# First layer norm's modulation weights loaded in four units of two feature tiles, with the first four projection tiles computed between the units

## The chip, the cores and the metric

The kernel runs on one core of one Trainium2 chip. The metric is device time in microseconds (us) of one execution; lower is better. Engines are named as in the profile: PE (TensorE, matmuls), PEld (its weight loads), DVE (VectorE), ACT (ScalarE), POOL (GpSimd) and SP (SyncE, which issues nearly all DMA transfers).

## The reference, cut to what matters

Two layers run over 256 latent tokens and 256 context tokens of width 1024. Each sub-layer begins with an RMS norm whose result is scaled and shifted by vectors that come from the conditioning vector `c` (latent tokens) or `c_ctx` (context tokens) through `mod_w`. This case is about the very first such norm and the projection `even_w_in` behind it:

```python
mod = silu(c) @ mod_w[0] + mod_b[0]          # 6 vectors of 1024: shift, scale, gate, shift, scale, gate
h   = x * rsqrt(mean(x * x) + EPS) * norm_g  # per token, over the 1024 features
h   = h * (1 + scale) + shift                # modulate
p   = h @ even_w_in                          # 1024 x 3328: a_q, a_k, a_v, b_q, b_ff, b_fb, b_i, b_g
```

The first projection tiles are the attention key and query (`a_k`, `a_q`), the value (`a_v`), then the inputs of the recurrent heads. Everything later (attention, recurrence, output projection, FFN, the second layer) stays as it is.

## The kernel before, in words

Features lie on the 128 partitions, tokens in the free dimension: 8 feature tiles k of 128 features by 512 tokens (latent 0:256, context 256:512). All dense products are done in three matmuls per weight block and feature tile: activations and weights are each split into a rounded part (`hi`) and the rest (`lo`), and hi*hi, lo*hi and hi*lo are added in PSUM. The split of activations gives the tiles `hh` and `hl`; the split of weights gives `whi` (ACT, line 268) and `wlo` (DVE, line 269). Weights arrive as pieces of 8 blocks of 128x128 (512 KB, tile `raw`) in the order in which `take` asks for them; `ensure` splits pieces up to LOOK = 2 ahead.

The program's first stage is written in a fixed order (`tc.manual_schedule`); there each engine runs its instructions in the order of the code. Before the change this stage does:

- SP loads constants, `x` (8 latent tiles of 128 KB, 4 context tiles of 256 KB), then `mod_w`'s columns for scale and shift of the first norm as 32 tiles of 256 KB: four quarters `nt` of 8 tiles (one for each feature tile of the contraction); the quarters are scale features 0:512, scale 512:1024, shift 0:512, shift 512:1024. Then come the first raw pieces.
- ACT and DVE square and sum `x`, PE sums over the partitions (line 453), ACT takes Ln and Exp for the reciprocal root: first for latent tokens, then for context tokens.
- `mod0a(nt)` (line 175) is 8 matmuls of fp32, which PE runs as 16 rows of the trace, on four column groups at once, followed by a copy to SBUF on ACT (line 178). `mod0b(nt)` (line 185) is 4 small matmuls (8 rows) that turn the result onto the partitions; `mod_finish` (lines 154 and 158, DVE) adds the bias and makes `gsv` = (1 + scale) * norm_g. A quarter of scale or shift serves four feature tiles.
- `Norm.scaled` (line 459, DVE) multiplies x by `gsv` and the root; `Norm.shifted` adds the shift and splits: `hh` on ACT (line 465), `hl` on DVE (line 466). All four quarters are done before the first `shifted`.

Behind this stage the work is ordered by `group`, which goes on PE in program order and gives, after every TICK = 1600 columns, one step to each lane (`q`: attention) and to the further modulation vectors (`mod_tick`, one task per MODE ticks; most tasks are two DVE reductions of 1.22 us, line 233). The group `p1` computes the output tiles a_k and a_q's first tile, for latent and context tokens apart (96 matmuls of 256 columns); `p2` computes the other three tiles of a_q and a_v (96 matmuls of 512 columns). `qk_post` (lines 567 and 578 on PE) follows a tile. `tokgroup` (lines 409 to 411) comes next with 96 matmuls of 512 columns.

Of the kernel before, what the change touches and what calls it, by code (L numbers as in the profile page):

```python
# [16 lines left out]
P = 128  # L17
D = 1024
# [22 lines left out]
MODE = 2.3  # L41
# [27 lines left out]
def hybrid_kernel(ctx, tc, xT, wst, mw0, mwT, small, cbc, cst, imask, dmat, out, order):  # L69
# [35 lines left out]
    x = [cp.tile([P, L], F32, tag=f"x{k}", name=f"x{k}") for k in range(KD)]  # L105
    xc = [u((P, 2, L)) for _ in range(KD // 2)]
    for k in range(KD):
        nc.sync.dma_start(x[k][:], xT[:, k, LAT])
    for k in range(KD // 2):
        nc.sync.dma_start(xc[k][:], xT[:, 2 * k:2 * k + 2, CTX])  # L110

    def xs(k, s):
        return x[k][:] if s == 0 else xc[k // 2][:, k % 2, :]

    con0 = [u() for _ in range(3)]
    mws = []
    for i in range(32):
        if 16 <= i < 22:
            if i % 2 == 0:
                pair = rawp.tile([P, 2, NT], F32, tag="raw", name=nm("raw"))  # L120
            t = pair[:, i % 2, :]
        elif 22 <= i < 28:
            if i % 2 == 0:
                pair = mp.tile([P, D], F32, tag="mr", name=nm("mr"))
            t = pair[:, (i % 2) * NT:(i % 2 + 1) * NT]
        elif i < 16:
            t = u()[:]
        else:
# [42 lines left out]
    def mod0a(nt):  # L171
        ps = axb()
        for k in range(KD):
            g = k % 4
            T.matmul(ps[32 * g:32 * g + 32, :], cT[:, k, :], mws[nt * 8 + k], start=(k < 4), stop=(k >= 4),  # L175
                     skip_group_check=True)
        parts[nt] = u()
        A.activation(parts[nt][:], ps[:], AF.Copy)

    def mod0b(nt):  # L180
        ch, half = 1 - nt // 2, nt % 2
        part = parts[nt]
# [3 lines left out]
        mod_finish(0, ch, half * 4, half * 4 + 4, ps2[:].rearrange("p c s -> p s c"))  # L186
# [73 lines left out]

    def ensure(p):
        for q in range(len(pieces), min(p + LOOK, N_PIECE - 1) + 1):
            r = q
            load_raw(r)
            src = raws.pop(r)
# [153 lines left out]
    class Norm:  # L419
# [6 lines left out]
        def pre(self, k):  # L426
# [5 lines left out]
            A.activation(hi[:, LAT], x[k][:], AF.Copy, scale=g)  # L432
            V.scalar_tensor_tensor(lo[:, LAT], x[k][:], g, hi[:, LAT].bitcast(F32), ALU.mult, ALU.subtract)
# [50 lines left out]

    manual[0] = True
    with tc.manual_schedule():
        h = new_h()
        ns = [Norm(0, 0, s, h) for s in range(2)]
        for n in ns:
            for k in range(KD):  # L490
                n.add(k)
            n.stats()
        for r in range(3):
            load_raw(r)
        ts_ = [u() for _ in range(KD)]
# [16 lines left out]
        mod0b(3)  # L512
        for i, t in enumerate(con0):
            nc.sync.dma_start(t[:], cst[:, N_KEEP + i * NT:N_KEEP + (i + 1) * NT])
        nc.sync.dma_start(con[:, C_RCOS:], cst[:, C_RCOS:N_KEEP])
        nc.sync.dma_start(msk[:], imask)
        nc.sync.dma_start(cb[:], cbc.rearrange("s d -> (s d)").unsqueeze(0).partition_broadcast(P).rearrange("p o (s d) -> p (o s) d", s=2))
        for n in ns:
            for k in range(KD):
                if n.s == 0 and k in (1, 4):  # L520
                    ensure(k // 4 - LOOK)
                n.shifted(k, ts_[k][:, n.sl])
# [9 lines left out]

    omh = cp.tile([P, 4], F32, tag="omh", name="omh")
    nomh = cp.tile([P, 4], F32, tag="nomh", name="nomh")
    lbh = cp.tile([P, 4], F32, tag="lbh", name="lbh")
    l0, l1 = sml[:, S_LB:S_LB + 4], sml[:, S_LB + 4:S_LB + 8]
    mx, e0, e1 = sm(4), sm(4), sm(4)
    V.tensor_tensor(mx, l0, l1, ALU.max)
# [775 lines left out]
```

## Time and profile before

| what | value |
|---|---|
| median of the runs | 1154.58 us (1154.38 to 1154.76, 3 runs) |
| profiled execution, its own time | 1153.62 us |
| its span in the trace | 1151.9 us |
| PE busy / weight loads / DVE / ACT | 1123.6 / 1002.4 / 766.5 / 554.1 us |
| mean granted TensorE clock | 0.996 of full speed |
| PE in the first 20 us | 2.2 us busy |

The span is the trace from first to last instruction; the 1.7 us between it and the execution's own time lie around it. PE's ends are modelled, so a busy PE is not PE at its peak. The window views below give busy time of each engine in a stretch, the granted clock (1.00 is the upper of TensorE's two levels, 2.4 GHz; 0.50 the lower, 1.2 GHz) and what the DMA engines moved.

### The profile page before, as it was taken

What the parts mean: (1) busy time and instruction counts of PE and PEld (TensorE: products, weight loads), DVE (VectorE), ACT (ScalarE), POOL (GpSimd) and SP (SyncE); (2) the same over time, 40 slices, a digit from 0 to 9 for tenths busy, and PEclk for the clock granted to TensorE, in tenths of its full rate; (3) what the DMA queues carried; (4) which work ended last, traced back from release to release, by engine and by line L of the source; (5) the groups of instructions that cost most, each with busy time, mean ns of one, the idle gap of its engine ahead of it and who ended that gap; (6) DMA issues with size and microseconds to landing.
All of it is one profiled execution on the core that took longest, in us unless ns stands there. A gap on an engine that the chain in (4) does not pass through costs nothing.

```text
span 1151.9 us, 18864 instructions
## 1 busy us (share of the span) xinstructions
PE 1123.6 (98%) x7514; PEld 1002.4 (87%) x7514; DVE 766.5 (67%) x1399; ACT 554.1 (48%) x948; POOL 20.8 (2%) x46
## 2 busy tenths in 40 slices
PE   3999999999999999999999998999999999999998
PEld 1777878888998888888888898999999999999998
DVE  3878699789889557347884568373646577555553
ACT  5776667573763322132232466454445657543441
POOL 0012000000000000000000000000000000000000
PEclk9999999999999999999999999999999999999999
DMA  9976212225327446236884323343424265655553
GB/s 333 343 231 183 92 58 72 96 89 163 112 86 261 147 147 213 81 128 215 314 300 139 98 86 116 112 134 116 139 101 146 92 198 161 194 183 184 183 183 109
DMA packets 56121, 182.46 MB, mean 158 GB/s; under 512 B 6368, under 2 KB 9824, under 8 KB 55904
## 3 DMA queue, kind: packets, MB, share of 16 engines
q1 hardware_dynamic: 53648, 176.45, 46.9%
q0 software_dynamic: 2240, 4.72, 1.7%
q8 instruction: 59, 0.97, 0.3%
q14 instruction: 30, 0.25, 0.1%
q10 hardware_dynamic: 144, 0.08, 0.0%
HBM read 177.56 MB, written 1.05 MB: 155 GB/s over the span
## 4 chain that ended last, share of the span: by engine, by line
PE 90%; DVE 6%; ACT 2%; issue 1%; DMA 1%; DVEq 0%; ACTq 0%; SPq 0%
PE mm L338 24%; PE mm L336 24%; PE mm L337 24%; PE ax L337 2%; PE ax L336 2%; PE ax L338 2%; DVE wlo L269 1%; PE ax L175 1%; PE ax L656 1%; PE ax L675 1%; PE ax L777 1%; DVE u L459 1%; PE mm L411 1%; PE mm L409 1%; PE mm L410 1%
## 5 line engine op out<-in xcount | busy, mean ns | idle before, releaser
L268 ACT ACTIVATE whi<-raw 128x1024 fp32r<-128x1024 f32 x230 | 243.2, 1058 | 385.9 <-PE mm L337 222.4
L269 DVE TENSOR_TENSOR wlo<-raw,whi 128x1024 fp32r<-128x1024 f32 x230 | 280.7, 1222 | 167.5 <-ACT whi L268 166.8
L336 PE MATMUL mm<-hh,whi 128*128 128x256 f32 (+1 forms) x1072 | 362.4, 339 | 1.2 <-ACT whi L268 0.9
L338 PE MATMUL mm<-hh,wlo 128*128 128x256 f32 (+1 forms) x1072 | 361.3, 337 | 0.6 <-DVE wlo L269 0.6
L337 PE MATMUL mm<-hl,whi 128*128 128x256 f32 (+1 forms) x1072 | 361.4, 337 | 0.1
L336 PE MATMUL mm<-u,whi 128*128 128x256 f32 (+2 forms) x768 | 236.3, 309 | 1.1 <-DVE x L483 1.1
L337 PE MATMUL mm<-u,whi 128*128 128x256 f32 (+2 forms) x768 | 236.9, 309 | 0.0
L338 PE MATMUL mm<-u,wlo 128*128 128x256 f32 (+2 forms) x768 | 236.7, 308 | 0.0
L338 PEld LDWEIGHTS mm<-hh,wlo 128*128 128x128 f32 x1072 | 204.3, 191 | 21.9 <-DVE wlo L269 0.8
L336 PEld LDWEIGHTS mm<-hh,whi 128*128 128x128 f32 x1072 | 204.1, 191 | 21.6 <-ACT whi L268 0.9
L337 PEld LDWEIGHTS mm<-hl,whi 128*128 128x128 f32 x1072 | 204.2, 191 | 20.2 <-DVE hl L466 0.3
L336 PEld LDWEIGHTS mm<-u,whi 128*128 128x128 f32 x768 | 146.4, 191 | 8.7 <-issue 1.3
L337 PEld LDWEIGHTS mm<-u,whi 128*128 128x128 f32 x768 | 146.6, 191 | 7.1
L338 PEld LDWEIGHTS mm<-u,wlo 128*128 128x128 f32 x768 | 146.5, 191 | 7.1
L233 DVE CUSTOM_DVE_ANT_0 mr<-mr,cb 128x1024 f32<-128x1024 f32 x72 | 87.1, 1222 | 16.1 <-DMA mr<-in_mwT_dram 15.4
L416 ACT ACTIVATE u<-u 128x512 fp32r<-128x512 f32 (+1 forms) x84 | 43.0, 526 | 46.9 <-DVE u L1002 26.9
L1002 DVE TENSOR_TENSOR u<-u,mm 128x512 f32<-128x512 f32 (+1 forms) x40 | 22.1, 553 | 43.2 <-PE mm L338 43.2
L417 DVE TENSOR_TENSOR u<-u,u 128x512 fp32r<-128x512 f32 (+1 forms) x84 | 46.5, 565 | 5.1 <-ACT u L416 5.1
L233 DVE CUSTOM_DVE_ANT_0 u<-mr,cb 128x1024 bf16<-128x1024 f32 x40 | 48.3, 1219 | 2.2 <-ACT cb L524 1.2
L336 PE MATMUL ax<-u,u 128*128 128x256 f32 x160 | 45.9, 287 | 3.1 <-ACT u L416 3.1
L483 DVE SCALAR_TENSOR_TENSOR x<-mm,modv,x 128x256 f32<-128x256 f32 x48 | 22.3, 480 | 36.1 <-PE mm L338 36.1
L337 PE MATMUL ax<-u,u 128*128 128x256 f32 x160 | 46.0, 287 | 0.0
(220 smaller groups left out, 1233.8 us busy)
## 6 DMA issues: line engine op xcount, KB each, us to landing
raw<-in_wst_dram SPq DMA_DIRECT2D x230, 512.0 KB, 3.6
mr<-in_mwT_dram SPq DMA_DIRECT2D x80, 512.0 KB, 4.5
u<-in_mw_dram SPq DMA_DIRECT2D x16, 256.0 KB, 5.2
u<-u POOLq DMA_DIRECT2D x20, 128.0 KB, 5.3
u<-in_dmat_dram POOLq DMA_DIRECT2D x8, 256.0 KB, 3.1
raw<-in_mw_dram SPq DMA_DIRECT2D x6, 256.0 KB, 5.2
mr<-in_mw_dram SPq DMA_DIRECT2D x6, 256.0 KB, 5.2
x<-in_xT_dram SPq DMA_DIRECT2D x8, 128.0 KB, 3.3
```

What stands on the lines that cost most here:

```text
L175: T.matmul(ps[32 * g:32 * g + 32, :], cT[:, k, :], mws[nt * 8 + k], start=(k < 4), stop=(k >= 4), skip_group_check=True)
L233: V.tensor_tensor_reduce(o, mr[:], cb[:, s, :], 1.0, 0.0, ALU.mult, ALU.add, mvec(l, s, ch, k))
L268: A.activation(hi[:], src[:], AF.Copy)
L269: V.tensor_tensor(lo[:], src[:], hi[:].bitcast(F32), ALU.subtract)
L336: T.matmul(o, w[0], a[0], start=first, stop=False, skip_group_check=shared)
L337: T.matmul(o, w[0], a[1], start=False, stop=False, skip_group_check=shared)
L338: anchor[0] = T.matmul(o, w[1], a[0], start=False, stop=last, skip_group_check=shared)
L409: T.matmul(ps[t][:], a[0], w[0], start=(k == 0), stop=False)
L416: A.activation(hi, src, AF.Copy)
L417: V.tensor_tensor(lo, src, hi.bitcast(F32), ALU.subtract)
L483: V.scalar_tensor_tensor(xs(m, s), ps[:, sl], mvec(l, s, ch, m), xs(m, s), ALU.mult, ALU.add)
L1002: V.tensor_tensor(g[:, 0:w], g[:, 0:w], ps[2 * i + 1][:, 0:w], ALU.mult)
```

## The change

The modulation weights of the first norm are regrouped on the host: unit p (of four) holds the scale columns and the shift columns of feature tiles 2p and 2p+1, so that after one unit two feature tiles can be finished. Unit 0 is now loaded ahead of `x`. The statistics use squares of 512 columns and two accumulating matmuls per stream, and one ACT table that holds both Ln and Exp. The first four output tiles (a_k and a_q's first three tiles, now all `p1`, 512 columns wide) are taken k by k inside the written order: `dense(k, ...)` with the three matmuls of each tile, `mod0a` and `mod0b` of the next unit between them. During this stage a weight piece (two k of four tiles) is split when its unit comes (`look[0] = 0`). The constants of the recurrent gates (`lb_consts`) move into the stage. `p2` keeps two tiles, and MODE goes from 2.3 to 1.5.

```diff
-MODE = 2.3
+MODE = 1.5
...
+    mw_load(0)
+    for j in range(2):
+        nc.sync.dma_start(xl[j][:], xT[:, 0, 4 * j:4 * j + 4, :])
     for k in range(KD // 2):
-        nc.sync.dma_start(xc[k][:], xT[:, 2 * k:2 * k + 2, CTX])
+        nc.sync.dma_start(xc[k][:], xT[:, 1, 2 * k:2 * k + 2, :])
...
+        for i, ch in enumerate((1, 0)):
+            mod_finish(0, ch, 2 * p, 2 * p + 2, ps2[:, 2 * i:2 * i + 2, :].rearrange("p c s -> p s c"))
...
-        mod0a(0)
-        mod0a(1)
-        mod0b(0)
-        scaled(0, range(4))
-        mod0a(2)
-        mod0b(1)
-        scaled(0, range(4, 8))
-        scaled(1, range(4))
-        mod0a(3)
-        mod0b(2)
-        scaled(1, range(4, 8))
-        mod0b(3)
...
+        load_raw(0)
+        for p in range(1, 3):
+            mw_load(p)
+            load_raw(p)
+            if p == 1:
+                mod0a(0)
+                mod0b(0)
+                lb_consts()
+                for n in ns:
+                    xx = xl if n.s == 0 else xc
+                    sq = []
+                    for j in range(4):
+                        q = u((P, 2, L))
+                        A.activation(q[:], xl[j // 2][:, 2 * (j % 2):2 * (j % 2) + 2, :] if n.s == 0 else xc[j][:], AF.Square)
+                        if j:
+                            V.tensor_tensor(sq[0][:], sq[0][:], q[:], ALU.add)
+                        sq.append(q)
+                    ps = axb()[:, 0:L]
+                    for j in range(2):
+                        T.matmul(ps, ones, sq[0][:, j, :], start=(j == 0), stop=(j == 1))
+                    n.r = u()[:, 0:L]
+                    A.activation(n.r, ps, AF.Ln, bias=epst[:], scale=1.0 / D)
+                    A.activation(n.r, n.r, AF.Exp, scale=-0.5)
...
+        def dense(k, js):
+            for j in js:
+                w = take('ein', k, j)
+                o = p1[j][:]
+                T.matmul(o, w[0], HS[k][0], start=(k == 0), stop=False)
+                T.matmul(o, w[0], HS[k][1], start=False, stop=False)
+                anchor[0] = T.matmul(o, w[1], HS[k][0], start=False, stop=(k == KD - 1))
+
+        for p in range(4):
+            k = 2 * p
+            ts = [scaled(k)]
+            ensure(p)
...
+            shifted(k, ts[0])
+            ts.append(scaled(k + 1))
+            shifted(k + 1, ts[1])
+            dense(k, range(4))
+            if p < 3:
+                mod0a(p + 1)
+            dense(k + 1, range(2))
+            if p < 3:
+                mod0b(p + 1)
+            dense(k + 1, range(2, 4))
...
-    p1 = group('ein', [E_AK, E_AQ], K8, HS, sls=(LAT, CTX))
     start('q', qk_post([(p1[0], 1, kt), (p1[1], 0, qt)]))
-    p2 = group('ein', [E_AQ + 1, E_AQ + 2, E_AQ + 3, E_AV], K8, HS, kouter=False)
-    start('q', qk_post([(p2[j], 0, qt) for j in range(3)]))
-    start('q', v_post(p2[3]))
+    start('q', qk_post([(p1[2], 0, qt), (p1[3], 0, qt)]))
+    p2 = group('ein', [E_AQ + 3, E_AV], K8, HS, kouter=False, banks=[axb(), mmb()])
+    start('q', qk_post([(p2[0], 0, qt)]))
+    start('q', v_post(p2[1]))
```

ACT's queue at the start of the changed program; line 172 copies `mod0a(0)`, 490 to 492 belong to `lb_consts`, 517 are squares of x, 525 and 526 are Ln and Exp of a stream:

```order
L160 ACTIVATE cT<-sml 128x8x2
...
L172 ACTIVATE u_177<-ax_168 128x512
L490 ACT_TABLE_LOAD
L491 ACTIVATE s_188<-s_188 128x4
L492 ACTIVATE s_189<-s_189 128x4
L517 ACTIVATE u_202<-x_86 128x512
...
L525 ACTIVATE u_216<-ax_213,eps 128x256
L526 ACTIVATE u_216<-u_216 128x256
L517 ACTIVATE u_219<-u_88 128x512
...
L525 ACTIVATE u_233<-ax_230,eps 128x256
L526 ACTIVATE u_233<-u_233 128x256
L263 ACTIVATE whi_261<-raw_148 128x1024
```

Before, the same queue began its squares (line 445) straight behind the two small Exps, and the copies of `mod0a` (line 178) stood behind both streams' Exp (line 456):

```order
L541 ACTIVATE s_413<-s_413 128x4
L542 ACTIVATE s_414<-s_414 128x4
L1037 ACTIVATE idr<-con 128x128
L445 ACTIVATE u_199<-x_86 128x256
...
L290 ACTIVATE u_253<-ax_251,eps 128x256
L456 ACT_TABLE_LOAD
L456 ACTIVATE u_253<-u_253 128x256
L178 ACTIVATE u_280<-ax_271 128x512
L178 ACTIVATE u_291<-ax_282 128x512
```

So the copy of `mod0a(0)` and the constants' Exps moved ahead of all squares.

PE's queue of the changed program at the end of unit 0; line 178 is `mod0b(1)`, lines 544 to 546 are `dense(1, ...)` with hh_134 and then `dense(2, ...)` with hh_136:

```order
L544 MATMUL mm_255<-hh_134,whi_261 128x512
L545 MATMUL mm_255<-hl_135,whi_261 128x512
L546 MATMUL mm_255<-hh_134,wlo_262 128x512
L178 MATMUL ax_329<-con,u_321 128x2 x4
L544 MATMUL mm_256<-hh_134,whi_261 128x512
L545 MATMUL mm_256<-hl_135,whi_261 128x512
L546 MATMUL mm_256<-hh_134,wlo_262 128x512
L544 MATMUL mm_257<-hh_134,whi_261 128x512
L545 MATMUL mm_257<-hl_135,whi_261 128x512
L546 MATMUL mm_257<-hh_134,wlo_262 128x512
L544 MATMUL mm_254<-hh_136,whi_346 128x512
L545 MATMUL mm_254<-hl_137,whi_346 128x512
```

Before, the last two `mod0b` (line 185) stood together, and the first dense matmuls (line 336) came right behind them:

```order
L185 MATMUL ax_341<-con,u_313 128x2 x4
L185 MATMUL ax_351<-con,u_339 128x2 x4
L336 MATMUL mm_431<-hh_183,whi_365 128x256
L336 MATMUL mm_432<-hh_183,whi_365 128x256
L337 MATMUL mm_431<-hl_184,whi_365 128x256
```

Each of the three later `mod0b` now has six dense matmuls behind it before the first matmul that needs its result.

DVE's queue at the same place of the changed program, from `mod_finish` of unit 1 (lines 147, 151) over `scaled` (454) and the piece's `wlo` (264) to `hl` (461):

```order
L147 TENSOR_TENSOR modv<-ax_329,sml 128x2x2
L151 SCALAR_TENSOR_TENSOR gsv<-modv,sml 128x2x2
L147 TENSOR_TENSOR modv<-ax_329,sml 128x2x2
L454 SCALAR_TENSOR_TENSOR u_343<-x_86,gsv,u_216 128x256
L454 SCALAR_TENSOR_TENSOR u_343<-u_89,gsv,u_233 128x256
L264 TENSOR_TENSOR wlo_347<-raw_166,whi_346 128x1024
L461 SCALAR_TENSOR_TENSOR hl_137<-u_343,modv,hh_136 128x256 x2
```

This sequence now stands once in every unit; before, `scaled` of all tiles stood ahead of the last `mod_finish`.

## Rows read from the trace of the kernel before

**Rows 1.** The page, first part: busy time, share of the span, instructions.

```profile
PE 1123.6 (98%) x7514; PEld 1002.4 (87%) x7514; DVE 766.5 (67%) x1399; ACT 554.1 (48%) x948; POOL 20.8 (2%) x46
```

**Rows 2.** The chain that ended last, first 45 us: start, us, what.

```profile
19.00 1.22 PE ax L453 x2
20.22 5.53 PE ax L175 x32
25.75 0.98 PE ax L185 x8
26.73 2.00 PE ax L175 x16
...
29.72 4.18 PE ax L175 x16
...
38.33 0.80 PE mm L338 x2
```

**Rows 3.** Timeline of PE, three stretches: start, us, line, operation, tiles, count.

```profile
50.73 0.40 PE L336 MATMUL mm<-hh,whi 128*128 128x512 f32 x1
...
75.20 0.39 PE L409 MATMUL mm<-whi,hh 128*128 128x512 f32 x1
...
78.38 0.39 PE L411 MATMUL mm<-whi,hl 128*128 128x512 f32 x1
78.61 2.73 PE L567 MATMUL ax<-u,u 128*128 128x512 f32 x6
...
87.33 1.69 PE L578 MATMUL ax<-u,u 128*128 128x256 f32 x6
```

**Rows 4.** DMA: an issue group (time to landing last), SP's timeline, a window.

```profile
con<-in_cst_dram SPq DMA_DIRECT2D x1, 129.0 KB, 2.6
...
7.00 10.65 SPq L130 DMA_DIRECT2D u<-in_mw_dram  x16
...
14.00:16.00 2.00, 0.00 (x0) 0.00 (x0) 0.55 (x2) 1.99 (x7) 0.00 (x0) 1.00 1.05 406
```

**Rows 5.** Timeline of ACT: Ln, Exp, a copy, a weight split, 12 of `hh`.

```profile
12.49 0.47 ACT L290 ACTIVATE u<-ax,eps 128x256 f32<-128x256 f32 x1 [1.82 <-PE ax L453]
...
14.28 0.42 ACT L456 ACTIVATE u<-u 128x256 f32<-128x256 f32 x1
...
23.93 0.60 ACT L178 ACTIVATE u<-ax 128x512 f32<-128x512 f32 x1 [1.48 <-PE ax L175]
...
37.68 1.04 ACT L268 ACTIVATE whi<-raw 128x1024 fp32r<-128x1024 f32 x1
38.63 4.89 ACT L465 ACTIVATE hh<-u,modv 128x256 fp32r<-128x256 f32 x12
```

**Rows 6.** Timeline of DVE: `mod_finish`, `scaled`, a weight split, 12 of `hl`, two 512-wide.

```profile
26.77 0.17 DVE L154 TENSOR_TENSOR modv<-ax,sml 128x8 f32<-128x8 f32 x1 [7.83 <-PE ax L185]
...
27.18 1.67 DVE L459 SCALAR_TENSOR_TENSOR u<-x,gsv,u 128x256 f32<-128x256 f32 x4
...
37.06 1.21 DVE L269 TENSOR_TENSOR wlo<-raw,whi 128x1024 fp32r<-128x1024 f32 x1
...
40.52 4.83 DVE L466 SCALAR_TENSOR_TENSOR hl<-u,modv,hh 128x256 fp32r<-128x256 f32 x12
...
61.78 1.42 DVE L573 SCALAR_TENSOR_TENSOR u<-u,sml,u 128x512 f32<-128x512 f32 x2 [2.53 <-ACT u L572]
```

**Rows 7.** Windows (PE, PEld, DVE, ACT, POOL busy, granted clock, DMA) and two PE waits.

```profile
36.60:41.20 4.60, 3.88 (x17) 3.47 (x18) 4.60 (x10) 4.60 (x11) 0.00 (x0) 0.63 1.03 411
...
706.90 0.58 PE L336 MATMUL ax<-u,u 128*128 128x256 f32 x1 [3.13 <-ACT u L416]
...
708.00:710.00 2.00, 2.00 (x11) 2.00 (x11) 2.00 (x3) 1.98 (x4) 0.00 (x0) 0.50 0.00 0
...
933.61 0.35 PE L336 MATMUL mm<-u,whi 128*128 128x256 f32 x1 [1.08 <-DVE x L483]
...
934.00:936.00 2.00, 2.00 (x19) 2.00 (x18) 1.71 (x5) 2.00 (x6) 0.00 (x0) 1.00 0.85 285
```

More of the change, by code (lines that the diff above doesn't have):

```diff
@@ L169, in hybrid_kernel, with mod0a @@
     parts = {}
-    def mod0a(nt):
+    def mod0a(p):
         ps = axb()
@@ L174, in mod0a, with mod0b @@
             g = k % 4
-            T.matmul(ps[32 * g:32 * g + 32, :], cT[:, k, :], mws[nt * 8 + k], start=(k < 4), stop=(k >= 4),
+            T.matmul(ps[32 * g:32 * g + 32, :], cT[:, k, :], mws[p][k][:], start=(k < 4), stop=(k >= 4),
                      skip_group_check=True)
[L177 to L182, printed above, removed]
+        parts[p] = u()
+        A.activation(parts[p][:], ps[:], AF.Copy)
+    def mod0b(p):
+        part = parts[p]
         ps2 = axb((P, 4, 2))
@@ L259, in load_raw @@
             raws[r] = t
+    look = [0]
     def ensure(p):
[L262 to L265, printed above, removed]
+        for q in range(len(pieces), min(p + look[0], N_PIECE - 1) + 1):
+            load_raw(q)
+            src = raws.pop(q)
             hi = wp.tile([P, PIECE, P], F32R, tag="whi", name=nm("whi"))
@@ L483, in upd, with lb_consts @@
         V.scalar_tensor_tensor(xs(m, s), ps[:, sl], mvec(l, s, ch, m), xs(m, s), ALU.mult, ALU.add)
+    omh = cp.tile([P, 4], F32, tag="omh", name="omh")
+    nomh = cp.tile([P, 4], F32, tag="nomh", name="nomh")
+    lbh = cp.tile([P, 4], F32, tag="lbh", name="lbh")
+    def lb_consts():
+        l0, l1 = sml[:, S_LB:S_LB + 4], sml[:, S_LB + 4:S_LB + 8]
+        mx, e0, e1 = sm(4), sm(4), sm(4)
+        V.tensor_tensor(mx, l0, l1, ALU.max)
+        V.tensor_tensor(e0, l0, mx, ALU.subtract)
+        V.tensor_tensor(e1, l1, mx, ALU.subtract)
+        A.preload_act_table_set("natural_log_exp_and_others")
+        A.activation(e0, e0, AF.Exp)
+        A.activation(e1, e1, AF.Exp)
+        V.tensor_tensor(e1, e0, e1, ALU.add)
+        V.reciprocal(e1, e1)
+        V.tensor_tensor(e0, e0, e1, ALU.mult)
+        V.tensor_scalar(omh[:], e0, -0.5, 0.5, ALU.mult, ALU.add)
+        V.tensor_scalar(nomh[:], e0, 0.5, -0.5, ALU.mult, ALU.add)
+        V.tensor_scalar(lbh[:], e0, 0.5, 0.5, ALU.mult, ALU.add)
     manual[0] = True
@@ L508, in hybrid_kernel @@
-        scaled(1, range(4))
-        mod0a(3)
-        mod0b(2)
-        scaled(1, range(4, 8))
-        mod0b(3)
[L513 to L522, printed above, removed]
@@ new lines, in hybrid_kernel, with scaled, shifted @@
+        HS = [(a[:], b[:]) for a, b in h]
+        p1 = [mmb() for _ in range(4)]
+        def scaled(k):
+            t = u()
+            for n in ns:
+                n.scaled(k, t[:, n.sl])
+            return t
+        def shifted(k, t):
+            for n in ns:
+                n.shifted(k, t[:, n.sl])
+        def dense(k, js):
[5 more added lines that the diff above has]
+                anchor[0] = T.matmul(o, w[1], HS[k][0], start=False, stop=(k == KD - 1))
@@ L524, in hybrid_kernel @@
         A.activation(cb[:], cb[:], AF.Silu)
+    look[0] = LOOK
     manual[0] = False
-    HS = [(a[:], b[:]) for a, b in h]
     K8 = list(range(8))
     E_AK, E_AQ, E_AV, E_I, E_H, E_G = 0, 1, 5, 6, 10, 22
[L533 to L538, printed above, removed]
```

74 lines of the change are left out of this document (24 added, 50 removed).

## The prediction, made before the changed kernel was run

> **What bounds the kernel now.** The page's first part comes first [rows 1]: PE is busy 98% of the span, the others far less, so time is won or lost only where PE waits or where PE rows are added. The chain that ended last is read next [rows 2]. In the first 38 us PE does little that counts: the second statistics matmul at 19.00, then four `mod0a` (5.53 for the first two, 2.00, 4.18) with 0.98 for a `mod0b`, and the dense stream runs from 38.33, when the first piece's `wlo` is there. Of the 28 us in which PE isn't busy 18 lie in the first 20 us (2.2 busy there), so the start of that stream, plus whatever is put into it later, sets the end. The chain also shows two speeds: two `mod0a` are 32 rows in 5.53, of which the second 16 take 2.00 like those at 26.73, so the first took 3.5. The window behind the start of the dense stream has a granted clock of 0.63 [rows 7]: most of it at the lower of the two levels, and before it PE had only small matmuls and waits.
>
> The point at which I compare both kernels is the start of `tokgroup`, before at 75.20 [rows 3]. Up to there PE has done p1, p2, two items' `qk_post` matmuls; the changed kernel has done the same by then, in another order, and the same work follows.
>
> **The change, part by part: the start.** SP's eight tiles of unit 0 now go behind `con`. `con` lands 2.6 us after its issue in the first us [rows 4], at about 3.4. A window in the middle of this load moves 406 GB/s, and 16 tiles of 256 KB are issued in 10.65 us; either gives 0.65 us a tile. Unit 0 is there at 3.4 + 8 x 0.65 = 8.6, all of x at 8.6 + 2.1 MB / 406 GB/s = 13.8. From there ACT's queue decides, and it is in order: copy of `mod0a(0)`, the two Exps of `lb_consts`, then the squares. The Exps need DVE rows that stand behind `mod_finish` of unit 0. So the squares wait for `mod0b(0)`:
>
> - `mod0a(0)` behind its last tile, 1.4 (an estimate: two rows at the lower clock): 10.0. Copy 0.60 [rows 5]: 10.6.
> - `mod0b(0)`: 0.98 at the upper clock [rows 2]; I take twice that, 2.0, since PE has done nothing before: 12.6.
> - six small DVE operations at 0.17 [rows 6] and two small Exps, 1.3: 13.9.
> - latent statistics: four 512-wide squares at 0.60 (the ACT copy of that width), the last add 0.71 (half of 1.42 [rows 6]), two matmuls at 1.22 (one took that at 19.00 [rows 2]), Ln 0.47, Exp 0.42 [rows 5]: 6.44. 20.3. The context squares stand behind that Exp, and take 6.44 again: 26.8.
> - `whi` 1.04 [rows 5], `wlo` 1.21, two `hl` at 0.40 (4.83 / 12) [rows 6]: 29.8; with some 0.4 of hand-overs 30.2.
>
> That is the counterpart of 38.33, so **8.1 us gained**. Bounds: 26.8 if `mod0b(0)` and the statistics run at the upper clock (1.0 and 2 x 1.2 less), 31.5 if each hand-over costs 0.1 more.
>
> **Between the units.** Before, all modulation matmuls lay ahead of 38.33. Now three `mod0a` (2.00 each at the upper clock) and three `mod0b` (0.98) lie inside the dense stream, where nothing covers them, since PE itself does them: 3 x 2.98 = **8.9 us**. Each `mod0b` also begins a wait. Let it end at 0. `mod_finish`, `scaled`, `wlo` and `hl` follow on DVE: the first `scaled` came 0.45 behind the end of a `mod0b` (26.73 to 27.18) with two operations between, now three: 0.55. Two `scaled` at 0.42 (1.67 / 4): 1.4. `wlo` 1.21 is written ahead of `hl`: 2.6. Two `hl` 0.80: 3.4. PE has six matmuls in hand at 0.227 (75.20 to 78.38 are 14 of them [rows 3]), 1.4, and one more that needs only `hh`, 0.23. It waits 3.4 - 1.6 = 1.8. Three times **5.4 us**. In the last unit two matmuls of p2 are drawn into the wait, less 0.45. The second tile of a unit is covered: 11 matmuls, 2.5 us, against 1.7 for two more `scaled` and `hl`. ACT's part (a copy 0.60, `whi` 1.04 ahead of time, four `hh` at 0.41) is hidden under DVE's; if it weren't, `hh` would be late by what ACT has queued, at most 1.04.
>
> **What hardly counts.** The 92 narrow matmuls from 38.33 to 50.73 took 12.4; 46 wide ones at 0.227 with the same 1.7 us lost to the clock ((1 - 0.63) x 4.6 [rows 7]) take 12.1: 0.3 gained. Transfers: unit 1 has landed by 20, unit 3 and its piece by 38, and they are wanted at 34 and 55; the pace is not DMA's. The first `qk_post` now has two further items' copies ahead of its Ln on ACT (four operations of 0.60), so its second matmuls (L578) may wait 0.5. MODE 1.5 with fewer ticks gives about as many modulation tasks up to `tokgroup`'s end: 24576 columns / 1600 / 1.5 = 10 against 40960 / 1600 / 2.3 = 11. They stand closer together on DVE, whose slack behind 38 us hides them; without that slack I'd give 2 us.
>
> **Sum.** 8.9 + 5.4 - 0.45 + 0.5 - 8.1 - 0.3 = 6.0 us slower. `tokgroup` should start near 81.2. Against the profiled execution's own 1153.62 that is 1159.6; the median of the runs is 1.0 above that execution, so 1160.6.
>
> **A rule weighed against the rows.** PE waited 1.08 before 933.61 and the window behind has the granted clock 1.00; it waited 3.13 before 706.90 and 708 to 710 has 0.50, the lower level [rows 7]. The waits between units are 1.8 us with a matmul inside, nearer to the first. So the sum has no clock loss there. The Trainium skill (TensorE: Matmul & The Clock Gate, section "HAM oscillation — how this bites in real kernels") tells of a tile loop that waits for data in every tile and loses the clock in every tile, which speaks against a stage in units; it would make the sum 11.2 in place of 6.0.
>
> **Rivals.**
> - *The clock falls in each unit.* Each fall costs 1.7 us, as behind 36.60. For it: a `mod0b` and a wait follow each other, and the fall before the dense stream also came behind `mod0b` and short waits. Against it: six full matmuls stand between. Three falls: 6.0 + 5.2 = 11.2, 1165.8.
> - *A shorter start.* With `mod0b(0)` and the statistics at the upper clock the stream begins at 26.8: 2.6 slower, 1157.2. For it: unit 0's matmuls come just before; against: they trickle in with the tiles.
> - *The squares don't wait* (the other side). If x's arrival alone set the statistics, the last square ends at 14.4, add, two matmuls, Ln and Exp at 18.4, `hh` and `hl` at about 20.6 with the piece split earlier. That is 17.7 ahead of 38.33: 9.6 better than the sum, so 3.6 faster, 1151.0. The sum changes sign at a start of 24.2. For it: the data is there; against: the written order of ACT and the 2.4 us of each pair of statistics matmuls.
> - *The change does what it is made for and no more*: a gain at the start that the units eat exactly, a start near 24, or waits of 0 for 1.8 (then 0.6 slower): within 0.2%.
>
> **How the numbers follow.** 0.2% is 2.3 us, about what a measurement of this kernel can tell from no change. Chances: forecast 0.60, clock falling 0.12, shorter start 0.12, no difference 0.09, faster 0.07. The predicted time is the forecast's, 1160.6. The range reaches down to just below the shorter start (1156.2) and up to the falling clock (1166.0); what is left out is the no-difference case, the faster one and a little above. Slower: 0.60 + 0.12 + 0.12 = 0.84.
>
> **What would show it right or wrong.** Right: the first `wlo` dense matmul near 30; ACT's first square near 14, not 11; three PE waits of about 1.8 us for `hl`, ten us apart, near 40, 50 and 60; `mod0a` rows of units 1 to 3 in 2.0 us each; `tokgroup` near 81. Wrong: a start of the stream before 27, a granted clock under 1.00 between 40 and 65, waits for DMA in units 1 to 3, or a different set of waits behind 100 us, where the order of lanes shifts by a few rows and the 3.13 us wait at 706.90 could change by about a us either way.

## The result, and the profile after

The changed kernel takes 1174.16 us (four runs, 1173.91 to 1174.70) against 1154.48 for the kernel before: ratio 1.0173, 95% interval 1.0157 to 1.0189. That is 19.7 us slower; the forecast was 6.0 slower, and the range ended at 1166.0. Times are medians of a kernel's executions; one of the four of e3_before_lag took 6266.66 us, counts as slow and is left out of its figures. The profiled execution has a span of 1172.0 us, 20.1 more than before.

First the page, with the rows that answer to [rows 1], and the granted clock in 40 slices:

```profile
PE 1132.6 (97%) x7470; PEld 1001.6 (85%) x7470; DVE 766.5 (65%) x1397; ACT 547.2 (47%) x936; POOL 20.8 (2%) x46
...
PEclk7999999999999999999999998999999999999999
```

PE is busy 9.0 us longer than before with 44 rows fewer, and idle 11 us more. Then the start, in the chain that ended last (start, us, what; compare [rows 2]):

```profile
5.19 6.07 PE ax L169 x15
...
17.47 2.09 PE ax L523 x4
...
23.92 2.09 PE ax L523 x4
...
34.32 1.85 PE ax L169 x16
...
37.76 0.80 PE ax L178 x8
```

and the rows of PE's timeline at which the dense stream begins, waits in the units, and reaches `tokgroup` (compare [rows 3]):

```profile
30.01 0.80 PE L545 MATMUL mm<-hl,whi 128*128 128x512 f32 x1 [0.46 <-DVE hl L461]
...
40.46 0.50 PE L544 MATMUL mm<-hh,whi 128*128 128x512 f32 x1 [0.41 <-ACT hh L460]
41.84 0.50 PE L545 MATMUL mm<-hl,whi 128*128 128x512 f32 x1 [0.88 <-DVE hl L461]
...
62.53 0.50 PE L545 MATMUL mm<-hl,whi 128*128 128x512 f32 x1 [0.88 <-DVE hl L461]
...
80.97 0.40 PE L404 MATMUL mm<-whi,hh 128*128 128x512 f32 x1
```

The stream begins at 30.0 (forecast 30.2). Each of the three later units costs 1.9 and 0.95 us of modulation matmuls and a wait of 0.9 for `hl`, the first two of them also 0.4 for `hh`. And `tokgroup` starts at 80.97 (forecast 81.2, before 75.20). So 5.8 us are lost up to there, and 14.3 behind it. Windows of PE (busy, count, granted clock, DMA) show that the units keep the upper clock, and that it falls further on:

```profile
20.00:30.00 10.00, 2.87 (x5) 0.50 1.04 413
30.00:35.00 5.00, 4.99 (x19) 0.67 1.05 409
35.00:105.00 70.00, 66.52 (x308) 1.00 0.67 198
...
110.00:115.00 5.00, 3.06 (x13) 0.68 0.71 189
```

The waits of PE behind `tokgroup`'s start, its larger ones, one fence:

```profile
105.09 0.64 PE L200 MATMUL ax<-mr,cT 128*32 128x256 f32 x8
...
111.94 1.08 PE L200 MATMUL ax<-mr,cT 128*32 128x256 f32 x8 [4.62 <-DMA mr<-in_mwT_dram]
...
214.43 0.50 PE L654 MATMUL ax<-u,u 128*128 128x512 f32 x1 [1.15 <-ACT u L672]
216.93 2.84 PE L703 MATMUL ax<-u,u 128*64 128x128 f32 x48 [1.00 <-DVE u L815]
...
378.09 0.50 PE L331 MATMUL mm<-hh,whi 128*128 128x512 f32 x1 [1.41 <-ACT u L1029]
...
727.25 0.58 PE L331 MATMUL ax<-u,u 128*128 128x256 f32 x1 [3.62 <-ACT u L411]
```

With four of 0.35 to 0.84 and one of 0.28 they come to 14.2 us; the kernel before has 5.0 there, 3.13 of it the wait of [rows 7]. The clock takes 1.6 us in 110 to 115 (5 us at 0.68) and 1.7 more than before around 730 (3.4 against 1.7). So 9.2 + 3.3 of the 14.3 are found; the other 1.8 is assigned to no row.

**The largest wait, followed back.** L200 is `mod_pe`, a modulation step that TensorE does itself, from two `mr` tiles. The second half waits for a transfer. SP's timeline, DVE's and ACT's for the same microseconds:

```profile
105.79 0.33 SPq L190 DMA_DIRECT2D mr<-in_mwT_dram  x1
```

```profile
105.61 1.23 DVE L264 TENSOR_TENSOR wlo<-raw,whi 128x1024 fp32r<-128x1024 f32 x1 [2.35 <-ACT whi L263]
106.75 1.22 DVE L227 CUSTOM_DVE_ANT_0 u<-mr,cb 128x1024 bf16<-128x1024 f32 x1
...
110.19 1.22 DVE L227 CUSTOM_DVE_ANT_0 mr<-mr,cb 128x1024 f32<-128x1024 f32 x1
```

```profile
104.52 1.06 ACT L263 ACTIVATE whi<-raw 128x1024 fp32r<-128x1024 f32 x1 [2.68 <-PE mm L406]
107.35 1.06 ACT L263 ACTIVATE whi<-raw 128x1024 fp32r<-128x1024 f32 x1 [1.78 <-PE mm L406]
108.43 1.28 ACT L282 ACT_TABLE_LOAD   x1
109.72 0.69 ACT L282 ACTIVATE u<-ax,eps 128x512 f32<-128x512 f32 x1
110.31 0.59 ACT L925 ACTIVATE u<-mm 128x512 f32<-128x512 f32 x1
```

`mr` has three buffers. Two are held by modulation tasks that DVE still has in its queue (L227, 106.75 to 111.3, behind a `wlo` that waited 2.35 us for ACT; the `whi` that it waited for, at 104.52, had itself waited 2.68 for a matmul of PE). The tile for the second half is only asked for when the first half has been read, at 105.79, and it lands 6.1 us later (4.5 in the median of these transfers in this kernel, so a part of the wait may be the DMA queue's). In the kernel before the same sixteen matmuls run without a wait, in a row of its PE:

```profile
96.04 1.07 PE L206 MATMUL ax<-mr,cT 128*32 128x256 f32 x16
```

The ACT rows above show a second lateness. Lane q (`qk_post`, then attention) is behind: its last logarithm and a table load stand ahead of the copy (L925) of `tokgroup`'s output. The first softmax row on ACT, in the kernel before and in the changed one, one fence each:

```profile
97.43 0.68 ACT L644 ACTIVATE u<-ax,s 128x512 f32<-128x512 f32 x1
```

```profile
123.30 0.69 ACT L672 ACTIVATE u<-ax,s 128x512 f32<-128x512 f32 x1
```

25.9 us later, of which 5.8 are the start's. The four output tiles taken in the units give lane q no ticks (5 instead of 10 before `tokgroup`), and the query tiles make one work item more.

### The profile page after: what moved, and what is told of

It reads as the page before. It is cut to its first block, busy times and chain, and to the rows that moved or that the text cites. A ratio compares the mean times of both kernels' runs of the same rounds, so it can differ in the third digit from the quotient of the medians.

```text
span 1172.0 us, 18745 instructions
## 1 busy us (share of the span) xinstructions
PE 1132.6 (97%) x7470; PEld 1001.6 (85%) x7470; DVE 766.5 (65%) x1397; ACT 547.2 (47%) x936; POOL 20.8 (2%) x46
## 4 chain that ended last, share of the span: by engine, by line
PE 87%; DVE 7%; ACT 3%; DMA 2%; issue 1%; DVEq 0%; ACTq 0%; SPq 0%
PE mm L331 23%; PE mm L332 23%; PE mm L333 23%; PE ax L331 2%; PE ax L332 2%; PE ax L333 2%; DVE wlo L264 2%; PE ax L169 1%; DMA mr<-in_mwT_dram 1%; ACT whi L263 1%; DVE hl L461 1%; DMA raw<-in_wst_dram 1%; PE ax L805 1%; PE ax L684 1%; PE mm L545 1%
## 5 line engine op out<-in xcount | busy, mean ns | idle before, releaser
L331 PE MATMUL mm<-hh,whi 128*128 128x512 f32 (+1 forms) x1016 | 344.9, 340 | 1.7 <-ACT u L1029 1.4
L332 PE MATMUL mm<-hl,whi 128*128 128x512 f32 (+1 forms) x1016 | 343.7, 338 | 0.0
L333 PE MATMUL mm<-hh,wlo 128*128 128x512 f32 (+1 forms) x1016 | 342.5, 337 | 0.0
L331 PEld LDWEIGHTS mm<-hh,whi 128*128 128x128 f32 x1016 | 193.7, 191 | 22.9 <-ACT u L1029 1.8
L333 PEld LDWEIGHTS mm<-hh,wlo 128*128 128x128 f32 x1016 | 193.7, 191 | 19.7
L332 PEld LDWEIGHTS mm<-hl,whi 128*128 128x128 f32 x1016 | 193.8, 191 | 19.1 <-issue 0.4
L227 DVE CUSTOM_DVE_ANT_0 mr<-mr,cb 128x1024 f32<-128x1024 f32 x72 | 86.9, 1222 | 18.5 <-DMA mr<-in_mwT_dram 17.9
L331 PE MATMUL ax<-u,u 128*128 128x256 f32 x160 | 46.2, 289 | 3.6 <-ACT u L411 3.6
L227 DVE CUSTOM_DVE_ANT_0 u<-mr,cb 128x1024 bf16<-128x1024 f32 x40 | 48.2, 1219 | 1.3 <-DMA mr<-in_mwT_dram 1.2
L332 PE MATMUL ax<-u,u 128*128 128x256 f32 x160 | 46.2, 289 | 0.0
L333 PE MATMUL ax<-u,u 128*128 128x256 f32 x160 | 45.8, 286 | 0.0
```

Of the source, the lines that this page charges most:

```text
L227: V.tensor_tensor_reduce(o, mr[:], cb[:, s, :], 1.0, 0.0, ALU.mult, ALU.add, mvec(l, s, ch, k))
L331: T.matmul(o, w[0], a[0], start=first, stop=False, skip_group_check=shared)
L332: T.matmul(o, w[0], a[1], start=False, stop=False, skip_group_check=shared)
L333: anchor[0] = T.matmul(o, w[1], a[0], start=False, stop=last, skip_group_check=shared)
```

## The experiments

Eighteen kernels ran, each beside the kernel before on the same chip. The kernel before had medians of 1153.2 to 1153.8 there, against 1154.48 beside the changed kernel, so what an edit gains is counted from what each kernel lies above the kernel before beside it (19.7 us for the changed kernel). A ratio's interval is some 1.7 us wide to either side. Two counters pace the background work: `cnt` holds the columns since the last tick, `tickn` the ticks since the last modulation task. "Mended counters" stands for `cnt[0], tickn[0] = 960, 2.0` behind `tokgroup`, the values that the kernel before has there; the changed kernel has 576 and 0.

### MODE, the counters, the buffer

**e1_mode23**: the changed kernel with the modulation's pace of before.

```
-MODE = 1.5
+MODE = 2.3
```

> The changed kernel with MODE back at 2.3. Theory A (the modulation tasks were pulled ahead of what DVE can do behind p1, so that a tile of modulation weights finds no free buffer and PE waits 4.6 us for its DMA near 107 us, with 1.6 us of lower clock behind): the wait is gone, about 6 us less, near 1168. Theory B (the cost behind tokgroup comes from the lanes and ticks standing at other places, whatever MODE is): the time stays within 2 us of 1174, with waits elsewhere.

1169.92 us, ratio 1.0139 [1.0124, 1.0154], a gain of 3.5 us, between the theories. The wait for `mr` is gone; others came: 1.58 at 164.68 (ACT) with a clock of 0.78 behind it, and 3.17 at 297.63 (DVE). Setting the number back doesn't set the timing back, since the ticks are fewer.

**e1_before_mode15**: the kernel before with that one number changed, the other way.

```
-MODE = 2.3
+MODE = 1.5
```

> The kernel before with MODE 1.5 alone. Theory A: DVE begins its modulation tasks at 48 us there, 20 us ahead of tokgroup's middle, so the tasks are pulled forward without a wait for weights: within 3 us of 1154.5. If MODE 1.5 by itself costs what the change lost behind tokgroup (13 us), it shows here as well: near 1165 or more.

1175.13 us, 1.0172 [1.0148, 1.0196]: alone it costs 21 us, as much as the whole change. The theory's 3 us fell. Its PE waits show the same `mr`:

```profile
82.54 1.08 PE L206 MATMUL ax<-mr,cT 128*32 128x256 f32 x8 [5.74 <-DMA mr<-in_mwT_dram]
84.12 1.02 PE L212 MATMUL ax<-con,u 128*128 128x2 f32 x4 [0.50 <-ACT u L209]
100.16 0.61 PE L212 MATMUL ax<-con,u 128*128 128x2 f32 x4 [2.34 <-ACT u L209]
```

**e1_phase**: the changed kernel with mended counters.

```
     tokgroup('ein', E_I, HS, itok_done)
+    cnt[0], tickn[0] = 960, 2.0
     modt[0] = MODT[0]
```

> The changed kernel with the two tick counters set, behind tokgroup, to the values that they have there in the kernel before (960 columns, 2.0 ticks). Theory B: the waits that the changed kernel has at 214 to 235, 308 and 378 us (5.7 us together, 0.4 in the kernel before) come from ticks at other columns, so most of them go: 4 to 6 us less, near 1169. Theory A: the wait near 107 us stays, and the others, which come from lanes that started later, stay: within 2 us of 1174.

1167.79 us, 1.0116 [1.0099, 1.0133]. The `mr` wait stays (4.93 at 112.62), and the waits at 214 to 235, 308 and 378 us are gone: 5.6 us for the rows at which lane steps and modulation tasks fall.

**e1_slots4**: the changed kernel with a fourth modulation buffer.

```
-    mp = ctx.enter_context(tc.tile_pool(name="mp", bufs=3))
+    mp = ctx.enter_context(tc.tile_pool(name="mp", bufs=4))
...
-    up = ctx.enter_context(tc.tile_pool(name="up", bufs=47))
+    up = ctx.enter_context(tc.tile_pool(name="up", bufs=45))
```

> The changed kernel with four buffers for modulation weights in place of three (two fewer of the general pool). Theory A: the fourth buffer takes the place of the one that waits, the 4.6 us wait near 107 us and the clock's fall are gone, about 6 us less, near 1168, MODE being the same. Theory B: no difference over 2 us.

1171.34 us, 1.0152 [1.0137, 1.0167], a gain of 2.1 us where some 6 were expected. No wait for `mr`, but the next group's first matmul now waits 3.63 us for ACT's copy (L925) at 111.56: the second lateness stood right behind the first.

### The start and the units

**e2_cover**: twelve dense matmuls behind `mod0b`, in place of six.

```
-            dense(k, range(4))
+            dense(k, range(2))
             if p < 3:
                 mod0a(p + 1)
-            dense(k + 1, range(2))
+            dense(k, range(2, 4))
             if p < 3:
                 mod0b(p + 1)
-            dense(k + 1, range(2, 4))
+            dense(k + 1, range(4))
```

> The changed kernel with the two products of the next unit's modulation moved six dense products earlier, so that twelve dense products in place of six stand between the second of them and the next unit. Theory A (the waits for hh and hl in the units are a chain of fixed length): three times 1.3 to 1.8 us of waits go, and tokgroup starts at 76.5 to 77.5 us (81.1 in the changed kernel). Rival (the chain is as late since ScalarE or VectorE are busy with whi and wlo): tokgroup at 80 to 81 us. Behind tokgroup nothing is changed, so by theory A the whole is 1170 us, and 1174 us if the wait for mr takes the time up.

1170.43 us in a single run, a gain of 2.9 us. The waits fall to 0.24 for `hl` alone, `tokgroup` starts at 77.66 (3.3 us earlier), and the end keeps most of it. The chain behind `mod0b` is of fixed length, as the prediction had it.

**e2_start**: `lb_consts()` moved behind the second unit; the squares of both streams ahead of both logarithms; the table load kept behind the copy of `mod0a(0)`.

```
-        A.preload_act_table_set("natural_log_exp_and_others")
...
                 mod0a(0)
+                A.preload_act_table_set("natural_log_exp_and_others")
                 mod0b(0)
-                lb_consts()
                 for n in ns:
...
+                for n in ns:
                     n.r = u()[:, 0:L]
...
             dense(k + 1, range(2, 4))
+            if p == 1:
+                lb_consts()
```

> The changed kernel with the gates' constants (two exponentials and what goes with them) moved behind the second unit, and the squares of both streams ahead of both logarithms. Theory A (the chain of ScalarE, VectorE and TensorE up to the first dense product is what sets it): the dense stream starts at 24 to 26 us in place of 30.0, and tokgroup at 75.5 to 77 us. Rival (the transfers are late: weights of the second unit): a wait for DMA in the units, tokgroup at 79 us or later. The whole: 1168 to 1170 us by theory A, where the wait for mr stays as it is.

1174.69 us in a single run: a miss. The stream begins at 25.25, 4.8 us earlier, as expected, but `tokgroup` at 79.97. The constants now stand on DVE between `mod_finish` and `scaled` of a unit, from 45.27 to 46.82, and so its `hh` comes some 1.5 us later. DVE's first row of the constants and the `scaled` behind them, then PE's timeline and two windows of it:

```profile
45.27 0.15 DVE L487 TENSOR_TENSOR s<-sml 128x4 f32<-128x4 f32 x1
...
46.82 0.48 DVE L454 SCALAR_TENSOR_TENSOR u<-x,gsv,u 128x256 f32<-128x256 f32 x1
```

```profile
48.29 0.49 PE L543 MATMUL mm<-hh,whi 128*128 128x512 f32 x1 [1.91 <-ACT hh L460]
49.67 0.50 PE L544 MATMUL mm<-hl,whi 128*128 128x512 f32 x1 [0.89 <-DVE hl L461]
```

```profile
35.00:48.00 13.00, 10.06 (x53) 1.00 0.81 323
48.00:58.00 10.00, 8.82 (x42) 0.83 0.15 52
```

Waits of 1.91 and 0.89 a matmul apart bring the clock to 0.83 for 10 us, 1.7 us: the rival of the falling clock, in one unit, where the waits come to 2.8 us.

**e2_phase_m18**: the changed kernel with `MODE = 1.8` and counters of 960 and 11.2, so that `mod_pe` comes in the first tick behind `tokgroup` and the later ticks fall as before.

```
-MODE = 1.5
+MODE = 1.8
...
+    cnt[0], tickn[0] = 960, 11.2
     modt[0] = MODT[0]
```

> The changed kernel with MODE 1.8 in place of 1.5, and behind tokgroup both counters set so that the first modulation task on TensorE is done in the first tick behind tokgroup and every later tick falls where it does in the kernel before. Theory A (of what is lost behind tokgroup, the wait for the modulation tile and its clock are one part, some 6 us, since the two products come up before VectorE has freed the buffers; the shifted ticks are the other, some 6 us): the wait of 4.6 us for mr is gone or under 1 us, the waits at 214 to 235, 308 and 378 us are gone, and what is left is the 5.9 us up to tokgroup: about 1161 us. Rival B (VectorE and ScalarE are late there whatever the counters say, as the fourth buffer showed): another wait of 3 to 5 us stands between 105 and 120 us with the clock below 0.9: about 1167 us.

1163.88 us, 1.0085 [1.0069, 1.0100], between the two. The `mr` wait and the low clock behind it are gone, 9.5 of the 19.7 us with them and the shifted ticks; 1.60 for L925 is left at 108.27.

**e2_best**: these three together.

> The three edits together: later start of the dense stream taken out, more dense products ahead of each unit, and the counters as in the run with MODE 1.8. If the gains add up: the dense stream from 25 us, tokgroup at 72 to 73 us (75.2 in the kernel before), and 1151 to 1153 us, that is 0.997 to 0.999 of the kernel before. Rival (what is gained ahead of tokgroup is given back behind it, since VectorE's and ScalarE's queues then come later against TensorE): 1155 to 1162 us.

1157.43 us, 1.0032 [1.0019, 1.0045]: `tokgroup` at 73.92, earlier than before, and still 3.7 us slower at the end. With the dense matmuls ahead of the units the moved constants cost less here: 7.2 us were gained at `tokgroup` over e2_phase_m18 and 6.5 kept (PE waits 0.57 and 0.89 in one unit, at 45 and 46.5 us). The profiled execution was the fastest of the five (1154.96 to 1159.55).

### Lane q

**e3_before_lag**: the kernel before; the lanes' first ten steps behind the first group are left out, modulation ticks go on.

```
     def step():
         mod_tick()
+        if lag[0]:
+            lag[0] -= 1
+            return
...
+    lag[0] = 10
     p2 = group('ein', [E_AQ + 1, E_AQ + 2, E_AQ + 3, E_AV], K8, HS, kouter=False)
```

> The kernel before with one thing changed: the lanes' first ten steps are left out after the first group (the modulation ticks go on as they did), so that lane q runs some 20 us late, as in the changed kernel. Theory A (lane q's lag makes ScalarE's order bad around the end of tokgroup): waits of 2 to 4 us for ScalarE's copy near 100 us and several of 0.5 to 1.5 us up to 380 us: 1160 to 1168 us. Rival (the lag is harmless, only the modulation products' place counts): within 2 us of the kernel before.

1157.44, 1159.28 and 1161.53 us in three executions, 1.0052 [1.0038, 1.0067]: some 6 us for the lag alone, just short of theory A and beyond the rival. Lane q's first softmax comes 15.4 us later than in the kernel before:

```profile
112.87 0.69 ACT L648 ACTIVATE u<-ax,s 128x512 f32<-128x512 f32 x1
```

The largest wait near 100 us is 1.15, not 2 to 4, for ACT's copy in `mod_pe` (99.06). The waits of the changed kernel at 214 to 225 us stand here too, in PE's timeline:

```profile
203.98 0.50 PE L630 MATMUL ax<-u,u 128*128 128x512 f32 x1 [1.14 <-ACT u L648]
206.47 2.84 PE L679 MATMUL ax<-u,u 128*64 128x128 f32 x48 [1.00 <-DVE u L791]
```

In e1_phase, whose lane is later still (first softmax at 124.51), they are gone. So not the lag alone makes them, but how lane and modulation tasks fall against each other.

**e3_lane**: the changed kernel with MODE 2.3, twice as many ticks in the second group (`TICK // 2`, counter and task counter begun at 384 and 5), and query tiles 2 to 4 as one item, so that `tokgroup` should find all as before.

```
-MODE = 1.5
+MODE = 2.3
...
-    start('q', qk_post([(p1[2], 0, qt), (p1[3], 0, qt)]))
+    cnt[0], tickn[0], tk[0] = 384, 5, TICK // 2
     p2 = group('ein', [E_AQ + 3, E_AV], K8, HS, kouter=False, banks=[axb(), mmb()])
-    start('q', qk_post([(p2[0], 0, qt)]))
+    tk[0] = TICK
+    start('q', qk_post([(p1[2], 0, qt), (p1[3], 0, qt), (p2[0], 0, qt)]))
```

> The changed kernel with everything that hangs on the counters put back to what it is in the kernel before at the start of tokgroup: MODE 2.3; the counter of modulation ticks begins at 5 and ticks come twice as often in the second group's two output tiles, so that as many ticks have gone by; and the second to fourth query tile are one work item of lane q again. Theory A (all that the change costs behind tokgroup comes from the ticks: the modulation products ahead of VectorE, and lane q some 20 us late, so that two table loads and a logarithm stand ahead of the copy that the next group waits for): no wait over 0.5 us between 81 and 300 us that the kernel before hasn't, and the 5.9 us of the start are all that is left, 1159 to 1161 us. Rival (ten ticks in half the time bring ScalarE and VectorE late themselves): a wait of 1 us or more ahead of or in tokgroup, 1163 us or more.

1169.83 us, 1.0135 [1.0121, 1.0149]: the rival. Ten ticks in half the time make DVE late itself: 1.14 and 1.23 for `wlo` at 84.42 and 87.31, and

```profile
102.64 2.93 PE L607 MATMUL ax<-u,u 128*128 128x256 f32 x6 [3.44 <-DVE u L602]
```

The edit didn't put lane q back: its first softmax comes only 4.1 us earlier than in the changed kernel. So this run is no clean test of theory A. On ACT:

```profile
119.19 0.68 ACT L673 ACTIVATE u<-ax,s 128x512 f32<-128x512 f32 x1
```

**e3_lane_best**: the same with the start of e2_best.

> The same counters and work items, with the two edits at the start (constants later and both streams' squares first; twelve dense products ahead of each unit). Those took 8.4 us off the start of tokgroup in the run of the three edits together. If they add up: 1151 to 1153 us, faster than the kernel before by 0.1 to 0.3%. Rival: 1155 us or more, with a new wait in the second group or tokgroup.

1159.96 us, 1.0051 [1.0032, 1.0070]; the same waits, 0.92, 1.24 and 2.83.

**e4_merge, e4_merge_m18, e4_merge_best**: only the one work item for query tiles 2 to 4, in the changed kernel, in e2_phase_m18 and in e2_best.

```
-    start('q', qk_post([(p1[2], 0, qt), (p1[3], 0, qt)]))
     p2 = group('ein', [E_AQ + 3, E_AV], K8, HS, kouter=False, banks=[axb(), mmb()])
-    start('q', qk_post([(p2[0], 0, qt)]))
+    start('q', qk_post([(p1[2], 0, qt), (p1[3], 0, qt), (p2[0], 0, qt)]))
```

> The changed kernel with one edit: the second to fourth query tile are one work item of lane q again, in place of two and one, so that the lane has five or six steps less to go; MODE stays 1.5. Theory A (two separate causes): the lane's part goes (no logarithm and table loads ahead of tokgroup's copies; the waits at 214 to 235 us change or go), but the wait of 4.6 us for mr near 112 us stays, since the modulation products still come up with VectorE behind: 1166 to 1171 us. Rival (the lane's lag is what makes VectorE late and so the cause of the wait for mr too): no wait for mr, 1160 to 1163 us.

> The run with MODE 1.8 and the counters set, and the query tiles as one work item as well. Theory A (the 1.6 us at 108 us and most of the waits at 210 to 220 us in that run were lane q's): those go, and the whole is 1159.5 to 1162 us, the kernel before and the 5.9 us of the start. Rival (what is left is more than waits of the lane): 1163 to 1165 us as in that run.

> The same with the two edits at the start. If what each took off adds up (8.4 us at the start, 2 to 3 us behind tokgroup): 1151 to 1154.5 us, the same as the kernel before or 0.2% faster. Rival (an earlier tokgroup finds ScalarE and VectorE late): 1156 us or more.

1175.35 (a single run), 1168.51 (1.0129 [1.0116, 1.0143]) and 1159.85 us (1.0059 [1.0045, 1.0073]): two of three are slower than without it, the first not better. The lane comes earlier (first softmax at 111.69 in e4_merge) and meets the modulation tasks: in each PE waits 1.63 for a copy of lane q (L643, L644) near `tokgroup`'s end, and then for `mr`, 3.37, 2.87 and 1.39. So taking some of the lag back doesn't take the wait for `mr` away; that part of the theory held, the gain did not.

### The buffer with mended counters

**e5_phase_slots4**, **e5_best_slots4** (the start of e2_best, MODE 1.5), **e5_mode15_slots4** (the kernel before, MODE 1.5): the fourth `mr` buffer, by the diff of e1_slots4, in each; the first two have e1_phase's line.

> The changed kernel with the counters set behind tokgroup (1167.8 us by itself, with only the wait of 4.9 us for mr and its clock left behind tokgroup) and a fourth buffer for the modulation tiles (45 work buffers in place of 47). Theory A (the buffer is the cause of that wait, and nothing else stands behind it once the ticks fall as before): the wait and the lower clock go, 1160 to 1162 us. Rival (ScalarE's queue is as late there as VectorE's: with the fourth buffer alone a wait of 3.6 us for ScalarE's copy took the place): 1165 to 1168 us.

> The same (MODE 1.5, counters 960 and 2.0, four buffers) with the two edits at the start, which took 8.4 us off the start of tokgroup. Theory A: 1151.5 to 1154 us. Rival (the wait for ScalarE's copy): 1156 to 1160 us.

> The kernel before with MODE 1.5 (1175.1 us) and the fourth buffer. Theory A (the buffer is the cause of its wait of 5.7 us for mr at 82.5 us and of the clock of 0.52 behind it, some 10 us together, and the lane does not lag here): 1158 to 1166 us. Rival (the products come too early for VectorE and ScalarE whatever the buffers, so that another wait of their results takes the place): 1170 us or more.

1166.05 (1.0104 [1.0088, 1.0119]), 1156.57 (1.0034 [1.0020, 1.0048]) and 1168.88 us (1.0131 [1.0116, 1.0146]). Nowhere does PE wait for `mr`. The first two are the rival's. The first is only 1.6 us better than e1_phase, because one wait takes the place of the other. It is the only one over 0.25 us between 81 and 700 us in e5_phase_slots4, on PE:

```profile
110.92 0.50 PE L331 MATMUL mm<-hh,whi 128*128 128x512 f32 x1 [3.63 <-ACT u L925]
```

In the third the buffer gave 6.1 of the 21 us back, between the theories; 2.10 and 2.35 for ACT's copy in `mod_pe` (L209) are left.

**e6_hold**: e5_best_slots4 with the lanes held in `tokgroup`'s last five steps, so that its copies stand ahead of the logarithm on ACT.

```
         mod_tick()
+        if hold[0]:
+            return
...
+                hold[0] = step_ >= KD + 3 - 5
                 work(NT)
```

> The fastest of the last three (four buffers, counters set, start mended) with the lanes' steps left out in the last five steps of tokgroup, so that on ScalarE the four copies of tokgroup's output stand ahead of lane q's logarithm and its two table loads. Theory A (what the next group waits for is the copy, late by the table load of 1.28 us and the logarithm of 0.69 us ahead of it): the wait of 3.63 us at 104 us falls by 2 us to 1.2 to 1.8 us, the clock there stays at 1.00, and the whole is 1152 to 1155 us. Rival (the copy waits for the cast of the weights ahead of it, which waits for TensorE): the wait stays above 3 us, 1156 to 1158 us; or the lane's further lag makes new waits behind it, 1157 us or more.

1156.99 us, 1.0032 [1.0021, 1.0044]. The wait fell by the 2.0 us of the table load and the logarithm, as expected. PE's row, then ACT's:

```profile
101.67 0.50 PE L334 MATMUL mm<-hh,whi 128*128 128x512 f32 x1 [1.63 <-ACT u L931]
```

```profile
101.04 1.55 ACT L931 ACTIVATE u<-mm 128x512 f32<-128x512 f32 x3
...
103.38 1.28 ACT L282 ACT_TABLE_LOAD   x1
```

The time did not fall (3.8 us above the kernel before, 3.0 in e5_best_slots4): waits of 0.77 and 0.35 at 290 to 292 us for ACT came in its place, and the rest isn't assigned. No version beat the kernel before.

## Why the prediction was wrong

**What held.** The start and the units. The squares waited for `mod0b(0)` and the constants, and the stream began at 30.0 (forecast 30.2). The first stream's statistics took 6.45 us (forecast 6.44), but by luck in part: three adds, not one, stood behind the squares, and the four matmul rows took 2.1 where two at 1.22 were counted. Modulation in the stream: 3 x (1.92 + 0.95) = 8.6 us (8.9). Waits: 1.3, 1.3 and 0.9, together 3.5 in place of 5.0: the chain from `mod0b`'s end to `hl` took 3.3 (3.4), but six matmuls and the one that needs only `hh` covered 2.0 of it, not 1.6. Of each wait of 1.3, 0.4 is for `hh`, which the forecast had in time. The wait at L606 didn't show. The clock was 1.00 from 35 to 105, so its rival fell for waits of this size. The page of the Trainium skill weighed there (TensorE: Matmul & The Clock Gate, section "HAM oscillation — how this bites in real kernels") tells of a loop that loses the clock in every tile; no unit of the changed kernel did, and a unit of e2_start with 2.8 us of waits did.

The sum at `tokgroup` was 6.0 and is 5.8, but its terms as measured (8.6 + 3.5 - 8.3, with the 0.3 as forecast) come to 3.5. So 2.3 us were not priced: some 0.6 since the stream's first 5 us run at 0.67 (before 2.9 us at 0.63), some 0.5 since the matmul behind each of five waits takes 0.1 more; the rest isn't assigned. The total was right in part by luck.

**The step that failed** is the one on MODE under "What hardly counts": that "about as many modulation tasks" come up, "closer together on DVE, whose slack behind 38 us hides them; without that slack I'd give 2 us". The count was right, ten tasks (and ten, not eleven, before), but the last two of the ten are one `mod_pe`, done on PE, which reads two `mr` tiles. It counts double and comes 2 x MODE ticks behind the task ahead of it, so 3 ticks in place of 4.6. What counts is not how busy DVE is in a mean but when it gets to the tasks that hold the buffers, and they stood behind a `wlo` that waited for ACT, and so for PE. Price: 4.62 and 1.6 of clock in the changed kernel. In the kernel before MODE 1.5 alone cost 21 us, of which the fourth buffer gave 6.1 back.

**The step that was given no number** is the order of lanes, which "shifts by a few rows", listed last and only as what would make the prediction wrong. Lane q came 20 us late against PE's work, not a few rows. A lag of 15.4 us by itself cost the kernel before some 6 us, and in the changed kernel the ticks' place (e1_phase) was worth 5.6. The start and units, the `mr` wait with its clock, and the ticks' place, 5.8 + 6.2 + 5.6, make 17.6 of the 20.1, taken as single effects.

**What is shown and what stays open.** Shown: the buffer is what PE waits for at 112 us (a fourth one takes the wait away three times), and ACT's order is the next thing (putting the copies ahead took 2.0 us off it). Not shown is that the causes add: together they gave 9.5 us in e2_phase_m18, of 6.2 and 5.6, and 7.2 in e5_phase_slots4, of 2.1 and 5.6, each measured figure good to some 2 us, and the edits that were to take lag back (e3_lane, e4_merge) made other results late. That a piece's weights are split only when its unit comes (`look[0] = 0`) is in every version of the changed kernel, and wasn't tried by itself. With the start mended `tokgroup` begins 0.2 to 1.5 us before the old one, and by the medians 4 to 8 us go behind it in each of the five orders that were tried. What costs them isn't settled. From `tokgroup`'s start to the end, one window of PE in the kernel before and one in e6_hold:

```profile
75.20:1151.90 1076.70, 1067.75 (x7215) 1.00 0.46 148
```

```profile
74.16:1155.00 1080.84, 1070.28 (x7215) 1.00 0.46 149
```

That is 4.1 us more for as many matmul rows: PE idles 1.6 us longer and is busy 2.5 longer. The clock doesn't explain the 2.5: over 40 us from 700 it is 0.96 in both, and in nearly all the rest at the upper level. No row was found that names them.

## What to carry to other kernels

Where background work is paced by counting foreground work, every edit that moves foreground work out of the count also moves the background work, and its effect on queues and buffers has to be priced as a change of its own: list what stands on each in-order engine around the next point where foreground and background meet. Slack of an engine is to be read at the instruction that frees a buffer, not as a busy share. And a wait that is first in a place can hide another of nearly its size (here 4.62 and 3.63), so look at what comes second before counting the gain.

## What was not expected of the hardware

A wait of nearly the same length, 3.1 to 3.6 us at the same matmul near 707 to 727 us, is followed by different clocks: over 40 us from 700 the granted clock was 1.00 in e2_best (wait 3.20), 0.96 in the kernel before (3.13) and 0.91 in the changed kernel (3.62) and in e3_lane (3.26), so 0 to 3.6 us are lost behind one wait. Whether this makes e2_best's spread (1154.96 to 1159.55) isn't shown, since only its fastest execution has a profile. In e2_best and in the changed kernel, one window of PE each:

```profile
700.00:740.00 40.00, 36.80 (x308) 1.00 0.42 130
```

```profile
700.00:740.00 40.00, 36.38 (x286) 0.91 0.33 104
```
